# Norm factors on all partitions: one product with ones and 32x32 turns on VectorE, in place of single-column and identity products

## The chip, the cores and the metric

The kernel runs on one core of one Trainium2 chip. The metric is device time in microseconds (us) of the whole execution, as the median of three runs. Engines are named as the profile does: PE is TensorE (PEld its weight loads), DVE VectorE, ACT ScalarE, POOL GpSimd, SP SyncE.

## The reference, cut to what matters

The program is one step of a two-layer decoder for a prompt of 1024 tokens and 8 samples of 8 tokens each. All is float32. The change touches two kinds of normalisation:

```python
def rmsnorm(x, g):
    xf = x.astype(F32)
    y = xf * lax.rsqrt(jnp.mean(xf * xf, axis=-1, keepdims=True) + NORM_EPS)
    return (y * g.astype(F32)).astype(x.dtype)
...
    # end of the RWKV-7 mixer, per token and head of 64
    mean = jnp.mean(o, axis=-1, keepdims=True)
    var = jnp.mean(jnp.square(o - mean), axis=-1, keepdims=True)
    o = ((o - mean) * lax.rsqrt(var + RW_GN_EPS) * p['ln_w'].reshape(RW_HEADS, HEAD_DIM).astype(F32)
         + p['ln_b'].reshape(RW_HEADS, HEAD_DIM).astype(F32))
```

`rmsnorm` stands ahead of both mixers and both FFNs, at the end of the Mamba-2 mixer (over 512 features) and at the end of the trunk.

## The kernel before

**Layout.** Features lie on the 128 partitions and tokens along the columns; a tensor of 1024 features is eight tiles. The tokens go in two halves: one of 576 columns (64 of the samples and 512 of the prompt, worked in the groups 0 to 320 and 320 to 576) and one of 512 columns (one group). A sum over features is thus a sum over partitions, which TensorE makes by a product, and the factor that comes out has to stand on all partitions again to multiply the tiles.

**Dense work.** Weights come by DMA, ScalarE rounds them to a high part `wh` (line 196) and GpSimd, or VectorE in the middle of the program, makes the low part `wl` (line 198). The activations are split in the same way into `hh` (ScalarE, line 218) and `hl` (line 219, VectorE for even tiles and GpSimd for odd ones). `mm3` multiplies in three products (lines 204 to 206) into one of four PSUM banks of the tag `acc`.

**A norm** is `rms` (lines 226 to 258). ScalarE squares the tiles and VectorE adds them up (line 239) into `ss`. For each block of 128 tokens (five for 576 columns, four for 512) one product of `ss` with a column of ones gives the sums, a token on each partition (line 245). VectorE takes the mean and adds epsilon (line 247), GpSimd raises to -0.5 (line 224, a power, one column a block), and for each block a product of the factor with the identity writes the factor on all partitions (line 255), into one PSUM bank for each group. `rms_split` then multiplies the eight tiles by factor and gain on VectorE (line 269), with the factor read from PSUM, and splits them. `rms` is called 13 times: eight times for the norms ahead of mixers and FFNs, twice at the end of the Mamba-2 mixer (tag `rk`, line 1485) and three times at the end (line 1525).

**The recurrence.** `Unit.finish` closes each of the 17 units of the RWKV-7 recurrence (256 columns): a product with the block matrix `blk` for the means (line 813), the difference on VectorE (814), the square on ScalarE (816), two products of the squares with the two columns `blk2` (820), the mean on VectorE (822), the power on GpSimd (224), a copy that spreads the four columns over 256 (824), two products with the identity (828) and the multiplication by the factor in PSUM (830). It runs beside other units' work; all of it shares two PSUM banks of the tag `rk`.

**What sets the order.** Generators are woven by hand: dense work yields, and the recurrence, attention or the norm of the other half takes its turn. Each engine then gets one fixed order of instructions, and an engine waits at the head of its own queue, whatever stands behind.

Of the kernel before, what the change touches and what calls it, by code (L numbers as in the profile page):

```python
# [19 lines left out]
P = 128  # L20
# [65 lines left out]
CC = {}  # L86
CN = []
for _pack, _items in enumerate(((("ident", 128), ("ones", 1), ("nhalf", 1)),
                                (("blk", 128), ("blk2", 2), ("maskp", 128), ("masks", 128), ("m2", 32), ("m4", 32), ("m8", 32),
                                 ("m16", 32), ("m1t", 32), ("i32", 32), ("bsel", 8)),  # L90
                                (("causal", 128), ("ssdmp", 128), ("ssdms", 64), ("bsel1", 8)),
                                (("smask", 256), ("pgtri", 128), ("sel", 32), ("hmask", 4), ("sub", 1)))):
    _n = 0
    for _name, _w in _items:
        CC[_name] = (_pack, _n, _w)
        _n += _w
    CN.append(_n)


def shape_constants():  # L100
    c = [np.zeros((P, n), np.float32) for n in CN]

    def put(name, a):
        a = np.asarray(a, np.float32)
        pack, n, w = CC[name]
        assert a.shape[1] == w
        c[pack][: a.shape[0], n:n + w] = a
# [5 lines left out]
    put("ones", np.ones((P, 1)))  # L113
    put("nhalf", np.full((P, 1), -0.5))
    put("blk", (r[:, None] // 64) == (r[None, :] // 64))
    put("blk2", (r[:, None] // 64) == np.arange(2)[None, :])
    strict = s[:, None] < t[None, :]
    incl = s[:, None] <= t[None, :]
    same = (s[:, None] // LS) == (t[None, :] // LS)
# [107 lines left out]
def rms(k, H, xs, width, groups=None, ft=None, tag="acc"):  # L227

    nc = k.nc
    ft = ft or (lambda: k.ft(H))  # L230
    groups = groups or H.groups
    lo, hi = groups[0][0], groups[-1][1]
    blocks = [b for b in H.blocks if lo <= b[1] < hi]
    ss = ft()[:, lo:hi]
    for i, x in enumerate(xs):
        sq = ft()[:, lo:hi] if i else ss
        nc.scalar.activation(sq, x[:, lo:hi], AF.Square)
        if i:
            nc.vector.tensor_add(ss, ss, sq)  # L239
        if i % 2:  # L240
            yield
    pt = k.bank(tag)
    nb = len(blocks)
    for j, (l, _, _) in enumerate(blocks):
        nc.tensor.matmul(pt[:, j:j + 1], ss[:, l - lo:l - lo + P], k.con("ones"), start=True, stop=True)  # L245
    r = k.bp.tile([P, 16], F32, name="rs", tag="rs", bufs=2)
    nc.vector.tensor_scalar(r[:, 8:8 + nb], pt[:, :nb], 1.0 / width, EPS, op0=ALU.mult, op1=ALU.add)
    rsqrt(k, r[:, 0:nb], r[:, 8:8 + nb])
    yield
    out = []  # L250
    for a, b in groups:
        pb = k.bank(tag)
        for j, (_, c, w) in enumerate(blocks):
            if a <= c < b:
                nc.tensor.matmul(pb[:, c - a:c - a + w], r[:, j:j + 1].to_broadcast([P, P]), k.con("ident")[:, :w], start=True, stop=True)  # L255
        out.append((a, b, pb[:, :b - a]))
    yield
    return out


def rms_split(k, H, xs, gname):
# [240 lines left out]
class Unit:  # L502
# [297 lines left out]
    def finish(self):  # L800
        m, cols, n, oo = self.m, self.cols, self.n, self.oo
        k = m.k
        nc = k.nc
        V, S = nc.vector, nc.scalar
        mm = nc.tensor.matmul

        def c3(t):
            return t.rearrange("p (c s) -> p c s", s=64)

        sg = self.et("sg")  # L810
        nc.sync.dma_start(sg[:, :n], k.zd[self.H.i][12][:, self.ts])
        pm = k.bank()
        mm(pm[:, 0:256], k.con("blk"), oo, start=True, stop=True)
        V.scalar_tensor_tensor(oo, pm[:, 0:256], -1.0 / 64, oo, op0=ALU.mult, op1=ALU.add)
        s2 = self.et("s2", 2)
        S.activation(s2, oo, AF.Square)
        yield
        pv = k.bank()
        for j in range(2):
            mm(pv[:, 2 * j:2 * j + 2], s2[:, 128 * j:128 * j + 128], k.con("blk2"), start=True, stop=True)  # L820
        r = m.tile([P, 8], "gr", 2)
        V.tensor_scalar(r[:, 4:8], pv[:, 0:4], 1.0 / 64, GN_EPS, op0=ALU.mult, op1=ALU.add)
        rsqrt(k, r[:, 0:4], r[:, 4:8])
        V.tensor_copy(c3(s2), r[:, 0:4, None].to_broadcast([P, 4, 64]))
        yield
        pr = k.bank()
        for j in range(2):
            mm(pr[:, 128 * j:128 * j + 128], s2[:, 128 * j:128 * j + 128], k.con("ident"), start=True, stop=True)
        for sl, i in cols:
            V.scalar_tensor_tensor(oo[:, sl], oo[:, sl], k.col("lnw", i), pr[:, sl], op0=ALU.mult, op1=ALU.mult)  # L830
        yield
        for sl, i in cols:
            V.scalar_tensor_tensor(oo[:, sl], oo[:, sl], k.col("lnb", i), self.bv[:, sl], op0=ALU.add, op1=ALU.add)
        yield
        pg = k.bank()
        for sl, i in cols:
            mm(pg[:, sl], m.g2[:, 128 * i:128 * i + 128], sg[:, :n], start=True, stop=True)
        V.scalar_tensor_tensor(oo, oo, 0.5, pg[:, 0:256], op0=ALU.mult, op1=ALU.mult)
        for sl, i in cols:
            nc.sync.dma_start(k.ysp0[self.H.i][4 + i][:, self.ts], oo[:, sl])  # L840
# [864 lines left out]
```

## Time and profile before

| | us |
|---|---|
| median of three runs | 3342.81 (3340.84 to 3344.05) |
| the profiled execution | 3342.04 |
| its span in the profile | 3340.3 |

| engine | busy us | share of the span |
|---|---|---|
| PE | 3169.4 | 95% |
| PEld | 2666.9 | 80% |
| DVE | 1906.4 | 57% |
| ACT | 1058.7 | 32% |
| POOL | 834.7 | 25% |

A busy time is the union of an engine's instructions. TensorE's instructions overlap in the records, so two of them are told apart by their starts. A product in float32 shows as two instructions in the trace.

### The profile page before, as it was taken

Reading aid. Unit: us, or ns where it says so; the run is one execution under the profiler, and the core shown is the slowest. Engines: PE = TensorE matmul, PEld = TensorE weight load, DVE = VectorE, ACT = ScalarE, POOL = GpSimd, SP = SyncE. Lnnn points to the kernel's source line nnn. Section 1 sums busy time; section 2 is a strip of 40 time slices with the busy share of each in tenths; the row PEclk is TensorE's granted clock in tenths of the full one; section 3 lists DMA queues with packets and bytes.
Section 4 is the critical chain, followed back from the end, with each engine's and each line's share of the span. In section 5 each row is a group of like instructions: output and inputs, shape, how many; then the busy total and the mean of one; then the engine's idle time right before and its main releaser. Section 6 shows DMA issues by size and latency. Waiting matters only on the chain. (4 is left out here: it accounts for less than half of the span.)

```text
span 3340.3 us, 63263 instructions
## 1 busy us (share of the span) xinstructions
PE 3169.4 (95%) x25213; PEld 2666.9 (80%) x25213; DVE 1906.4 (57%) x3643; ACT 1058.7 (32%) x2083; POOL 834.7 (25%) x561
## 2 busy tenths in 40 slices
PE   7999999999999998999999998989999998999998
PEld 7887667777889997977677675766777776899998
DVE  6766646565544447556655457565545656554445
ACT  4333323332222223345322223332224553322222
POOL 4423333332333333301300103002010001333332
PEclk9999999999999998999999999999999999999999
DMA  5322333211122234544345656775554334232222
GB/s 178 116 59 79 87 96 118 73 59 56 51 66 83 83 108 148 191 151 135 108 135 163 199 154 213 240 221 175 172 171 138 113 110 135 87 105 81 83 83 78
DMA packets 238471, 409.20 MB, mean 123 GB/s; under 512 B 37632, under 2 KB 129664, under 8 KB 238176
## 3 DMA queue, kind: packets, MB, share of 16 engines
q10 hardware_dynamic: 63232, 218.80, 20.2%
q1 hardware_dynamic: 165584, 152.27, 15.4%
q0 software_dynamic: 9360, 34.08, 3.0%
q8 instruction: 199, 3.26, 0.4%
q14 instruction: 96, 0.79, 0.1%
HBM read 352.23 MB, written 52.81 MB: 121 GB/s over the span
## 5 line engine op out<-in xcount | busy, mean ns | idle before, releaser
L204 PE MATMUL acc<-hh,wh 128*128 128x320 f32 (+2 forms) x3720 | 1264.9, 341 | 17.6 <-ACT hh L218 14.7
L206 PE MATMUL acc<-hh,wl 128*128 128x320 f32 (+2 forms) x3720 | 1255.4, 338 | 7.4 <-POOL wl L198 6.5
L205 PE MATMUL acc<-hl,wh 128*128 128x320 f32 (+2 forms) x3720 | 1254.8, 338 | 7.2 <-DVE hl L219 5.4
L204 PEld LDWEIGHTS acc<-hh,wh 128*128 128x128 f32 x3720 | 712.3, 192 | 97.5 <-ACT hh L218 19.4
L198 POOL TENSOR_TENSOR wl<-wraw,wh 128x1024 fp32r<-128x1024 f32 x225 | 539.6, 2398 | 1000.6 <-ACT wh L196 924.7
L196 ACT CAST wh<-wraw 128x1024 fp32r<-128x1024 f32 (+1 forms) x398 | 416.0, 1045 | 1139.4 <-PE acc L205 1054.1
L206 PEld LDWEIGHTS acc<-hh,wl 128*128 128x128 f32 x3720 | 712.8, 192 | 74.7 <-issue 11.1
L205 PEld LDWEIGHTS acc<-hl,wh 128*128 128x128 f32 x3720 | 713.0, 192 | 72.1 <-DVE hl L219 9.1
L205 PE MATMUL acc<-hidl,wh 128*128 128x320 f32 (+2 forms) x1056 | 353.1, 335 | 0.6 <-DVE hidl L219 0.6
L893 DVE TENSOR_TENSOR x<-x,acc 128x320 f32<-128x320 f32 (+2 forms) x528 | 270.3, 527 | 139.1 <-PE acc L206 136.1
L206 PE MATMUL acc<-hidh,wl 128*128 128x320 f32 (+2 forms) x1056 | 349.5, 332 | 0.0
L204 PE MATMUL acc<-hidh,wh 128*128 128x320 f32 (+2 forms) x1056 | 348.9, 337 | 0.4 <-ACT hidh L218 0.4
L198 DVE TENSOR_TENSOR wl<-wraw,wh 128x1024 fp32r<-128x1024 f32 x173 | 210.9, 1219 | 145.3 <-ACT wh L196 143.2
L1297 POOL DMA_INDIRECT kv<-in_cv,vidx x64 | 75.5, 1180 | 628.8 <-DVE kt L1249 134.4
L204 PEld LDWEIGHTS acc<-hidh,wh 128*128 128x128 f32 x1056 | 198.7, 189 | 24.0 <-issue 4.2
L205 PEld LDWEIGHTS acc<-hidl,wh 128*128 128x128 f32 x1056 | 199.2, 189 | 19.1 <-issue 2.2
L206 PEld LDWEIGHTS acc<-hidh,wl 128*128 128x128 f32 x1056 | 199.5, 189 | 15.6 <-issue 1.4
L219 DVE TENSOR_TENSOR hidl<-ft,hidh 128x512 fp32r<-128x512 f32 (+2 forms) x148 | 178.7, 1207 | 55.9 <-ACT hidh L218 55.8
L881 DVE SCALAR_TENSOR_TENSOR ft<-ft,acc 128x320 f32<-128x320 f32 (+2 forms) x132 | 70.1, 531 | 213.1 <-PE acc L206 212.9
L875 DVE SCALAR_TENSOR_TENSOR ft<-ft,acc 128x320 f32<-128x320 f32 (+2 forms) x132 | 69.7, 528 | 177.0 <-ACT ft L874 176.8
L218 ACT CAST hidh<-ft 128x512 fp32r<-128x512 f32 (+2 forms) x148 | 75.1, 507 | 117.5 <-DVE ft L881 114.3
L1249 DVE STREAM_TRANSPOSE kt<-kv 128x1024 f32<-128x1024 f32 x64 | 79.3, 1239 | 33.8 <-DMA kv<-in_ck 29.9
(339 smaller groups left out, 3334.7 us busy)
## 6 DMA issues: line engine op xcount, KB each, us to landing
wraw<-in_wi ACTq DMA_DIRECT2D x100, 512.0 KB
wraw<-in_wg ACTq DMA_DIRECT2D x88, 512.0 KB
wraw<-in_wu ACTq DMA_DIRECT2D x88, 512.0 KB
wraw<-in_wd ACTq DMA_DIRECT2D x88, 512.0 KB
kv<-in_ck SPq DMA_DIRECT2D x512, 64.0 KB
wraw<-in_wo ACTq DMA_DIRECT2D x32, 512.0 KB
ka<-kp SPq DMA_DIRECT2D x48, 128.0 KB
x<-in_xT SPq DMA_DIRECT2D x16, 288.0 KB
```

The source lines that it names most:

```text
L196: nc.scalar.copy(wh, raw)
L198: k.low.tensor_sub(wl, raw, wh)
L204: mm(acc, wh, xh, start=first, stop=False)
L205: mm(acc, wh, xl, start=False, stop=False)
L206: mm(acc, wl, xh, start=False, stop=last)
L218: k.nc.scalar.copy(hh, v)
L219: (eng or k.nc.vector).tensor_sub(hl, v, hh)
L875: nc.vector.scalar_tensor_tensor(s[:, a:b], s[:, a:b], 1.0, pc, op0=ALU.add, op1=ALU.mult)
L881: nc.vector.scalar_tensor_tensor(s[:, a:b], s[:, a:b], 0.5, pu, op0=ALU.mult, op1=ALU.mult)
L893: nc.vector.tensor_add(xs[n][:, a:b], xs[n][:, a:b], acc[:, :b - a])
L1249: V.transpose(kt, kr)
L1297: nc.gpsimd.indirect_dma_start(out=v, out_offset=None, in_=A["cv"].rearrange("o (s r) c -> (o s) (r c)", r=2), in_offset=bass.IndirectOffs ...
```

## The change

In `rms` one product for each group, with ones in all 128x128 weights and `ss` as the moving side, writes the sums on every partition, a token in each column. VectorE transposes the PSUM bank in 32x32 blocks into `ss`, so that the tokens of a block of 32 stand on the 32 partitions of each quadrant, in one column. Mean and power then work on 18 columns (576 tokens) or 16 (512), all four quadrants alike, in place of five or four. `turn_back` transposes these columns, each read 32 times over, into an SBUF tile `rb`, where the factor stands on all partitions; the multiplications of lines 269, 1485 and 1525 read it from there. `finish` does the same with `blk` as the weights, and eight columns in place of four; its copy and its four small products go, and its multiplication reads SBUF. The constant `blk2` goes.

```diff
-    pt = k.bank(tag)
-    nb = len(blocks)
-    for j, (l, _, _) in enumerate(blocks):
-        nc.tensor.matmul(pt[:, j:j + 1], ss[:, l - lo:l - lo + P], k.con("ones"), start=True, stop=True)
-    r = k.bp.tile([P, 16], F32, name="rs", tag="rs", bufs=2)
-    nc.vector.tensor_scalar(r[:, 8:8 + nb], pt[:, :nb], 1.0 / width, EPS, op0=ALU.mult, op1=ALU.add)
-    rsqrt(k, r[:, 0:nb], r[:, 8:8 + nb])
+
+    nb = (hi - lo) // 32
+    for a, b in groups:
+        pt = k.bank(tag)
+        nc.tensor.matmul(pt[:, :b - a], k.con("ones").to_broadcast([P, P]), ss[:, a - lo:b - lo], start=True, stop=True)
+        nc.vector.transpose(ss[:, a - lo:b - lo], pt[:, :b - a])
+    r = k.bp.tile([P, 36], F32, name="rs", tag="rs", bufs=2)
+    nc.vector.tensor_scalar(r[:, 18:18 + nb], ss[:, 0::32], 1.0 / width, EPS, op0=ALU.mult, op1=ALU.add)
+    rsqrt(k, r[:, 0:nb], r[:, 18:18 + nb])
     yield
-    out = []
-    for a, b in groups:
-        pb = k.bank(tag)
-        for j, (_, c, w) in enumerate(blocks):
-            if a <= c < b:
-                nc.tensor.matmul(pb[:, c - a:c - a + w], r[:, j:j + 1].to_broadcast([P, P]), k.con("ident")[:, :w], start=True, stop=True)
-        out.append((a, b, pb[:, :b - a]))
+    rb = k.bp.tile([P, 576], F32, name="rb", tag="rb", bufs=1)
+    turn_back(k, rb[:, 0:hi - lo], r[:, 0:nb])
     yield
-    return out
+    return [(a, b, rb[:, a - lo:b - lo]) for a, b in groups]
+
+
+def turn_back(k, out, r):
+
+    n = out.shape[1] // 32
+    k.nc.vector.transpose(out.rearrange("p (b s) -> p b s", s=32), r[:, :, None].to_broadcast([P, n, 32]))
...
         pv = k.bank()
-        for j in range(2):
-            mm(pv[:, 2 * j:2 * j + 2], s2[:, 128 * j:128 * j + 128], k.con("blk2"), start=True, stop=True)
-        r = m.tile([P, 8], "gr", 2)
-        V.tensor_scalar(r[:, 4:8], pv[:, 0:4], 1.0 / 64, GN_EPS, op0=ALU.mult, op1=ALU.add)
-        rsqrt(k, r[:, 0:4], r[:, 4:8])
-        V.tensor_copy(c3(s2), r[:, 0:4, None].to_broadcast([P, 4, 64]))
+        mm(pv[:, 0:256], k.con("blk"), s2, start=True, stop=True)
+        V.transpose(s2, pv[:, 0:256])
+        r = m.tile([P, 16], "gr", 2)
+        V.tensor_scalar(r[:, 8:16], s2[:, 0::32], 1.0 / 64, GN_EPS, op0=ALU.mult, op1=ALU.add)
+        rsqrt(k, r[:, 0:8], r[:, 8:16])
         yield
-        pr = k.bank()
-        for j in range(2):
-            mm(pr[:, 128 * j:128 * j + 128], s2[:, 128 * j:128 * j + 128], k.con("ident"), start=True, stop=True)
+        turn_back(k, s2, r[:, 0:8])
         for sl, i in cols:
-            V.scalar_tensor_tensor(oo[:, sl], oo[:, sl], k.col("lnw", i), pr[:, sl], op0=ALU.mult, op1=ALU.mult)
+            V.scalar_tensor_tensor(oo[:, sl], oo[:, sl], k.col("lnw", i), s2[:, sl], op0=ALU.mult, op1=ALU.mult)
```

The order of instructions moves with it. On TensorE at the first norm of the program (576 columns), before; `acc_324` and `acc_328` are the banks of the factor, `acc_378` and `acc_411` those of the first dense tile:

```order
L245 MATMUL acc_315<-con0_222,ft_246 128x1 x5
L255 MATMUL acc_324<-con0_222,rs_321 128x64
L255 MATMUL acc_324<-con0_222,rs_321 128x128 x2
L255 MATMUL acc_328<-con0_222,rs_321 128x128 x2
L204 MATMUL acc_378<-hh_230,wh_374 128x320
L204 MATMUL acc_411<-hh_230,wh_374 128x256
L205 MATMUL acc_378<-hl_238,wh_374 128x320
L206 MATMUL acc_378<-hh_230,wl_376 128x320
```

The same place after (lines of the changed kernel: 203 to 205 are 204 to 206 of before); `wh_484` is the weight of a second dense tile:

```order
L244 MATMUL acc_315<-ft_246,con0_222 128x320
L244 MATMUL acc_318<-ft_246,con0_222 128x256
L203 MATMUL acc_373<-hh_230,wh_369 128x320
L203 MATMUL acc_406<-hh_230,wh_369 128x256
L203 MATMUL acc_488<-hh_230,wh_484 128x320
L203 MATMUL acc_521<-hh_230,wh_484 128x256
L204 MATMUL acc_373<-hl_238,wh_369 128x320
L205 MATMUL acc_373<-hh_230,wl_371 128x320
```

The two banks of the factor are gone from the norm, and a second dense tile, which before could begin only when one of them was free again, begins with the first.

On VectorE at the end of a unit of the first recurrence, before; `gr` is the factor, `s_3878` the tile of the squares, the other rows belong to the next units:

```order
L822 TENSOR_SCALAR gr<-rk 128x4
L558 SCALAR_TENSOR_TENSOR cum<-reset,e 128x256
L824 COPY s_3878<-gr 128x256
L568 TENSOR_TENSOR e<-cum,e 128x256
L665 TENSOR_TENSOR tt<-tt,rk 128x128
```

The same place after (569, 657 and 666 are 568, 656 and 665 of before, 820 and 825 are 822 and 830):

```order
L818 STREAM_TRANSPOSE s_3862<-rk 128x256
L666 TENSOR_TENSOR tt<-tt,rk 128x128
L820 TENSOR_SCALAR gr<-s_3862 128x8
L569 TENSOR_TENSOR e<-cum,e 128x256
L657 STREAM_TRANSPOSE t_4143<-tt 128x128
L666 TENSOR_TENSOR tt<-tt,rk 128x128
L259 STREAM_TRANSPOSE s_3862<-gr 128x256
L818 STREAM_TRANSPOSE s_3928<-rk 128x256
L657 STREAM_TRANSPOSE t_4164<-tt 128x128
L820 TENSOR_SCALAR gr<-s_3928 128x8
L825 SCALAR_TENSOR_TENSOR oo<-oo,pp,s_3862 128x256
```

One instruction stood between the mean and what waits for the power; now there are three, and the multiplication follows on VectorE alone, four rows later.

On VectorE at the end of the program (the last 256 columns of the trunk's last norm), before, from the mean of the first group on:

```order
L247 TENSOR_SCALAR rs<-acc 128x3
L239 TENSOR_TENSOR ft<-ft 128x256
L893 TENSOR_TENSOR x<-x,acc 128x256
L239 TENSOR_TENSOR ft<-ft 128x256
L1525 SCALAR_TENSOR_TENSOR x<-x,pp,acc 128x320 x2
L893 TENSOR_TENSOR x<-x,acc 128x256 x2
L1525 SCALAR_TENSOR_TENSOR x<-x,pp,acc 128x320 x6
L239 TENSOR_TENSOR ft<-ft 128x256 x3
L247 TENSOR_SCALAR rs<-acc 128x2
L1525 SCALAR_TENSOR_TENSOR x<-x,pp,acc 128x256 x8
```

And after (237, 888 and 1520 are 239, 893 and 1525 of before):

```order
L245 STREAM_TRANSPOSE ft<-acc 128x320
L237 TENSOR_TENSOR ft<-ft 128x256
L247 TENSOR_SCALAR rs<-ft 128x10
L888 TENSOR_TENSOR x<-x,acc 128x256
L259 STREAM_TRANSPOSE rb<-rs 128x320
L888 TENSOR_TENSOR x<-x,acc 128x256
L1520 SCALAR_TENSOR_TENSOR x<-x,pp,rb 128x320
L888 TENSOR_TENSOR x<-x,acc 128x256
L1520 SCALAR_TENSOR_TENSOR x<-x,pp,rb 128x320 x7
L237 TENSOR_TENSOR ft<-ft 128x256 x3
L245 STREAM_TRANSPOSE ft<-acc 128x256
L247 TENSOR_SCALAR rs<-ft 128x8
```

Two turns came in for each of the two groups, and the second of them, which needs the power, stands on VectorE ahead of the last two additions.

## Rows read from the trace of the kernel before

**Rows 1.** The page of the profile: its span, and busy time of each engine with its share of the span and its instructions.

```profile
span 3340.3 us, 63263 instructions
...
PE 3169.4 (95%) x25213; PEld 2666.9 (80%) x25213; DVE 1906.4 (57%) x3643; ACT 1058.7 (32%) x2083; POOL 834.7 (25%) x561
```

**Rows 2.** Busy time by stretch (from:to, length, then busy us and instructions of TensorE, its weight loads, VectorE, ScalarE and GpSimd; granted clock of TensorE, DMA share, GB/s). 40 to 960 holds the two recurrences; 960 to 1255 is dense work alone.

```profile
40.00:960.00 920.00, 863.70 (x10402) 707.19 (x10401) 557.54 (x1398) 296.36 (x733) 301.08 (x237) 0.96 0.27 82
960.00:1255.00 295.00, 295.00 (x2168) 291.81 (x2167) 127.74 (x218) 73.49 (x110) 110.60 (x46) 1.00 0.27 89
```

**Rows 3.** The waits of TensorE (line waited for: us in total, times, longest us).

```profile
PE acc L255 <- POOL rs L224: 12.1, 8, 2.4
...
PE rk L828 <- DVE s L824: 3.7, 3, 2.8
...
PE rk L255 <- POOL rs L224: 2.8, 2, 1.7
```

**Rows 4.** The timeline of all engines at the norm of the last FFN, 2880 to 2900 (start us, us, engine, line, operation, tiles, shapes, count; in brackets the idle time ahead and what ended it).

```profile
2883.05 2.47 DVE L239 TENSOR_TENSOR ft<-ft 128x576 f32<-128x576 f32 x1 [1.13 <-ACT ft L237]
...
2885.58 2.29 PE L245 MATMUL acc<-con,ft 128*128 128x1 f32 x10 [4.11 <-DVE ft L239]
2887.91 0.17 DVE L247 TENSOR_SCALAR rs<-acc 128x5 f32<-128x5 f32 x1 [2.38 <-PE acc L245]
2888.15 1.17 POOL L224 TENSOR_TENSOR rs<-rs,con 128x5 f32<-128x5 f32 x1 [3.24 <-DVE rs L247]
...
2891.06 0.55 DVE L269 SCALAR_TENSOR_TENSOR ft<-x,pp,acc 128x320 f32<-128x320 f32 x1 [2.99 <-PE acc L255]
...
2893.83 1.78 DVE L269 SCALAR_TENSOR_TENSOR ft<-x,pp,acc 128x320 f32<-128x320 f32 x4
...
2894.03 1.42 POOL L219 TENSOR_TENSOR hl<-ft,hh 128x576 fp32r<-128x576 f32 x1 [4.71 <-ACT hh L218]
...
2896.20 1.78 DVE L269 SCALAR_TENSOR_TENSOR ft<-x,pp,acc 128x320 f32<-128x320 f32 x4
```

**Rows 5.** The products of one norm and of one recurrence unit on TensorE's own timeline, with the engine busy on both sides (columns as in rows 4). A product in float32 stands as two rows' worth: x8 are four products. Rows overlap, so what one takes from the engine is read from start to start.

```profile
2928.42 0.95 PE L245 MATMUL acc<-con,ft 128*128 128x1 f32 x8
2929.23 0.39 PE L204 MATMUL acc<-hidh,wh 128*128 128x320 f32 x1
...
2935.68 1.05 PE L255 MATMUL acc<-con,rs 128*128 128x128 f32 x8
2936.49 0.39 PE L204 MATMUL acc<-hh,wh 128*128 128x320 f32 x1
...
224.58 0.59 PE L813 MATMUL rk<-oo,con 128*128 128x256 f32 x2
225.01 1.05 PE L622 MATMUL rk<-krz,kb 128*128 128x128 f32 x8
```

**Rows 6.** The reciprocal square roots on GpSimd, line 224: min/median/max ns, the first and the last start, and the forms.

```profile
L224 POOL TENSOR_TENSOR gr<-gr,con x17: 1006/1016/1336, 240.9 to 949.2; 128x4 f32<-128x4 f32 x17
L224 POOL TENSOR_TENSOR rs<-rs,con x13: 695/1047/2101, 21.1 to 3331.4; 128x4 f32<-128x4 f32 x6, 128x5 f32<-128x5 f32 x5, 128x3 f32<-128x3 f32 x1, 128x2 f32<-128x2 f32 x1
```

**Rows 7.** Groups of VectorE by line and shape: the 32x32 transposes that are there already, and two lines of the unit's end (count | busy us, mean ns | idle ahead, and what ended it).

```profile
L1249 DVE STREAM_TRANSPOSE kt<-kv 128x1024 f32<-128x1024 f32 x64 | 79.3, 1239 | 33.8 <-DMA kv<-in_ck 29.9 <-issue 2.9 <-DMA kp<-hidh 1.0
...
L656 DVE STREAM_TRANSPOSE t<-tt 128x128 f32<-128x128 f32 x66 | 19.2, 299 | 0.4
...
L824 DVE COPY s<-gr 128x256 f32<-128x256 f32 x17 | 9.3, 549 | 13.4 <-POOL gr L224 13.4
...
L830 DVE SCALAR_TENSOR_TENSOR oo<-oo,pp,rk 128x256 f32<-128x256 f32 x16 | 7.6, 478 | 6.3 <-PE rk L828 6.1
```

**Rows 8.** VectorE's timeline at three norms of 512 columns: the last sum of squares, and the first product with the factor (columns as in rows 4).

```profile
1514.56 0.68 DVE L239 TENSOR_TENSOR ft<-ft 128x512 f32<-128x512 f32 x1
...
1518.91 0.75 DVE L269 SCALAR_TENSOR_TENSOR ft<-x,pp,acc 128x512 f32<-128x512 f32 x1 [1.98 <-PE acc L255]
...
2033.36 0.68 DVE L239 TENSOR_TENSOR ft<-ft 128x512 f32<-128x512 f32 x1
...
2039.28 1.41 DVE L269 SCALAR_TENSOR_TENSOR ft<-x,pp,acc 128x512 f32<-128x512 f32 x2 [3.29 <-issue]
...
2286.90 0.68 DVE L239 TENSOR_TENSOR ft<-ft 128x512 f32<-128x512 f32 x1
...
2294.34 0.75 DVE L269 SCALAR_TENSOR_TENSOR ft<-x,pp,acc 128x512 f32<-128x512 f32 x1 [5.45 <-PE acc L255]
```

**Rows 9.** VectorE's timeline at the end of the program (columns as in rows 4).

```profile
3324.04 1.01 DVE L1525 SCALAR_TENSOR_TENSOR x<-x,pp,acc 128x320 f32<-128x320 f32 x2 [1.07 <-PE acc L255]
...
3328.55 1.47 DVE L239 TENSOR_TENSOR ft<-ft 128x256 f32<-128x256 f32 x3
...
3333.45 3.22 DVE L1525 SCALAR_TENSOR_TENSOR x<-x,pp,acc 128x256 f32<-128x256 f32 x8 [2.09 <-PE acc L255]
```

**Rows 10.** Two lines of VectorE with min/median/max ns, line 269 (one input in PSUM) and line 365 (both in SBUF); and an addition of two SBUF tiles beside a subtraction of GpSimd on the timeline of all engines.

```profile
L269 DVE SCALAR_TENSOR_TENSOR ft<-x,pp,acc x96: 461/538/748, 24.0 to 2899.9; 128x320 f32<-128x320 f32 x32, 128x256 f32<-128x256 f32 x32, 128x512 f32<-128x512 f32 x32
...
L365 DVE SCALAR_TENSOR_TENSOR ft<-up,pp,ft x16: 731/748/2719, 153.1 to 1258.5; 128x512 f32<-128x512 f32 x16
...
2876.17 2.41 POOL L198 TENSOR_TENSOR wl<-wraw,wh 128x1024 fp32r<-128x1024 f32 x1 [3.99 <-ACT wh L196]
...
2876.66 2.54 DVE L239 TENSOR_TENSOR ft<-ft 128x576 f32<-128x576 f32 x1 [1.12 <-ACT ft L237]
```

More of the change, by code (lines that the diff above doesn't have):

```diff
@@ L88 @@
 for _pack, _items in enumerate(((("ident", 128), ("ones", 1), ("nhalf", 1)),
-                                (("blk", 128), ("blk2", 2), ("maskp", 128), ("masks", 128), ("m2", 32), ("m4", 32), ("m8", 32),
+                                (("blk", 128), ("maskp", 128), ("masks", 128), ("m2", 32), ("m4", 32), ("m8", 32),
                                  ("m16", 32), ("m1t", 32), ("i32", 32), ("bsel", 8)),
@@ L115, in shape_constants @@
     put("blk", (r[:, None] // 64) == (r[None, :] // 64))
-    put("blk2", (r[:, None] // 64) == np.arange(2)[None, :])
     strict = s[:, None] < t[None, :]
@@ L232, in rms @@
     lo, hi = groups[0][0], groups[-1][1]
-    blocks = [b for b in H.blocks if lo <= b[1] < hi]
     ss = ft()[:, lo:hi]
@@ L805, in finish @@
         mm = nc.tensor.matmul
-        def c3(t):
-            return t.rearrange("p (c s) -> p c s", s=64)
         sg = self.et("sg")
```

## The prediction

> **What bounds the kernel now.** I read the page first. TensorE is busy for 3169.4 of 3340.3 us, VectorE for 1906.4 [rows 1]: TensorE sets the time, and an edit counts by what it takes out of TensorE's own row or out of its gaps, 171 us in all. The busy time by stretch says where the gaps are: none in 295 us of dense work alone, 920.0 - 863.7 = 56 us in the two recurrences, where the ends of the 17 units lie [rows 2]. The rest is at norms and at the end of the program. The waits of TensorE name the edited lines: 12.1 us at the identity products of the norms for GpSimd's power, 2.8 us at those of the two Mamba norms, 3.7 us in the units for the spreading copy [rows 3]. Then the timeline of one norm that nothing covers [rows 4]: from the end of the last addition (2883.05 + 2.47 = 2885.52) to the first multiplication with the factor at 2891.06 pass 5.54 us, through TensorE, VectorE, GpSimd and TensorE again, and no dense work can start. Such a chain counts by its length, not by the work in it. So there are three kinds of places: norms beside other work, norms that are bare, and the units.
>
> **The products, beside other work.** With TensorE busy on both sides, eight instructions of the single-column products take 2929.23 - 2928.42 = 0.81 us and eight of the identity products 0.81 us, as their starts show [rows 5]: a single column costs what 128 columns cost. One product of 256 columns takes 225.01 - 224.58 = 0.43 us, so 512 columns take 0.86 and 576 take 0.97 by the same rate. A norm of 512 columns goes from 1.62 to 0.86 us (saves 0.76), one of 576 from ten and ten instructions, 2.02, to 0.97 (saves 1.05). Five norms have dense work on both sides (near 68, 664, 1692, 2820 and 2929 us): 3 x 0.76 + 2 x 1.05 = 4.4 us. At 1692 and 2820, the Mamba norms, nothing on TensorE needs the factor any more, so their 2.8 us of waiting go too [rows 3]. Sum: **-7.2 us**.
>
> **The units.** Eight instructions (0.81 us) become one product of 256 columns (0.43): 17 x 0.38 = 6.5 us. TensorE's 3.7 us of waiting for the copy go, since the factor no longer passes through it. Against that stands VectorE, whose results the same units wait for. The power costs GpSimd 0.695 us for the fewest columns, two, 1.006 at least for four [rows 6], 1.17 for five [rows 4]; that is a line, about 0.39 + 0.155 a column, so eight columns take 1.63, sixteen 2.87 and eighteen 3.18 us. No row shows more than five columns. The bounds are 1.17 (no growth) and 3.2 (the line); I take the line, since all shapes lie near it. A transpose takes 0.299 us for 128 and 1.239 for 1024 columns [rows 7], so 0.17 + 1.05 ns a column: 0.44 for 256, 0.50 for 320, 0.70 for 512, 0.77 for 576. None here reads PSUM or one column 32 times over; a multiplication with an input in PSUM runs 0.738 us for 512 columns and one of SBUF alone 0.748 at the median (lines 269 and 365), so I take the same price, and 0 to twice as the bound. VectorE now spends on the units 9.3 us in copies, 13.4 waiting for the power and 6.3 waiting for the identity products [rows 7], 29 us. After: two transposes, 17 x 0.88 = 15 us, and a wait for the power of 1.63 + 0.1, less two instructions of other units that stand between on average (about 0.6 us), 17 x 1.1 = 19 us. That is 34 us, 5 more. VectorE is at six tenths in this stretch (557.5 of 920 us, [rows 2]), so I let half of it reach TensorE: +2.5 us, between 0 and 5. Sum: -6.5 - 3.7 + 2.5 = **-7.7 us**.
>
> **The bare norms.** Six chains stand bare: 576 columns near 21, 1264 and 2888 us, 512 near 1516, 2036 and 2289. At 2888 TensorE runs at half pace (2.29 us for ten instructions, [rows 4]), so the new chain is: gap 0.06, products 2 x 0.97 = 1.94, gap and the second transpose 0.49 (the first lies under the second product), gap and mean 0.22, gap and power 0.07 + 3.18, gap and turn 0.05 + 0.77. That makes 6.8 us against 5.54. Before, the second group came 0.4 us behind the first, and now both are there at once, so the first finished tile is late by +0.8 us; I take this for all three. For 512 columns at full pace: 0.06 + 0.86 + 0.75 + 0.22 + 2.94 + 0.75 = 5.6 us. The old chains, from the last addition's end to the first multiplication, were 3.67 (1515.24 to 1518.91), 5.24 (half pace: 6.4 against it) and 6.76 us, where GpSimd and other products stood between [rows 8]: +1.9, +1.2, -1.1. At the end VectorE itself is the path. It waited 1.07 us for the factor of the first group [rows 9]. Now it makes two turns of 320 columns (0.84 in sequence) and waits about 1.5 for a power of ten columns (1.94): +1.3. For the last group a product at half pace (0.86), 0.49, 0.22, power of eight 1.70, turn 0.49 make 3.8 us against 3.43 (3328.55 + 1.47 = 3330.02 to 3333.45): +0.3. Sum: 2.4 + 2.0 + 1.6 = **+6.0 us**. If the power did not grow, the same sum would be about -6.
>
> **The place of the factor.** It moves from PSUM to SBUF. Line 269 with the factor in PSUM never took over 748 ns in 96 runs; line 365, both inputs in SBUF, has a median of 748 and a longest of 2719 ns, and a VectorE addition of two SBUF tiles took 2.54 us beside a GpSimd subtraction of 2.41 [rows 10]. So the multiplications become stoppable by GpSimd, which in each of eight norms makes four subtractions of `hl` (1.42 us at 2894.03, [rows 4]) while VectorE multiplies. The Trainium skill has this as a rule ("SBUF — State Buffer", "Who interferes with whom"): a VectorE instruction with two SBUF inputs and a GpSimd instruction that reads SBUF exclude each other for a whole instruction. The trace agrees with it by the two rows just named; it is the rule that speaks against this change, and the time by it is the first rival's. Against it stands the order on TensorE: the factor's banks are free, a second dense tile starts at once, and so TensorE has twice the work for each `hl` that comes. I put **+2 us** on it.
>
> **Sum:** -7.2 - 7.7 + 6.0 + 2 = -6.9 us on 3342.04, the profiled execution: 3335.1. That run lies 0.77 under the median of the three, so 3335.9; I say **3336**.
>
> **Rivals.** *VectorE stopped by GpSimd decides; slower.* A pair of tiles leaves the norm every 2896.20 - 2893.83 = 2.37 us [rows 4]; with a subtraction of 1.42 in line it is 3.8. Dense work takes TensorE 295.00 / 2168 = 0.136 us a product [rows 2]; a pair is 12 products in one dense tile, 1.6 us of work, and 3.2 in two. If the second tile's weights are not there in time, TensorE waits; at half of 4 x 1.42 in six norms that is 17 us: 3336 + 17 = 3353. For it: the durations in [rows 10]; against it: the order on TensorE, and TensorE at half pace after such a gap. It decides from the point where a pair takes longer than the tiles in hand. *The power is nearly flat; clearly faster.* At 1.17 us the bare norms gain 12 us, the units some 4 more: 3320. For it: from three to four columns it grew little; against it: two to five columns. The PSUM banks that come free would add to this. *The units don't feel it.* If the recurrences are paced by their own chain and not by TensorE's queue, the -7.7 goes and the rest is +0.8: about 3343.
>
> **How the numbers follow.** A run of this kernel can tell about 0.2% (6.7 us, so 3336.1 and 3349.5) from no change. The forecast, with 3328 to 3344 around it, has a chance of 0.50, and as its middle lies on the line it gives 0.28 to faster and 0.22 to the same. The stopped VectorE has 0.23 (0.18 slower, 0.05 same), the flat power 0.17 (faster), the units that don't feel it 0.10 (same). Faster 0.45, same 0.37, slower 0.18. The range reaches to the middles of the outer rivals: 3318 to 3353.
>
> **What the profile of after would show.** The power of 16 and 18 columns at 2.9 and 3.2 us, of eight at 1.6. Chains from the last addition to the first multiplication of 6.8 and 5.6 us. No wait of TensorE at a power. Transposes of 0.44 to 0.77 us. TensorE's busy time down by 6 us or more in 40 to 960, with gaps of 56 us or less. The forecast is wrong if the power is under 2 us, if multiplications at line 269 stretch to 1.5 us and more with TensorE waiting for `hl` behind them, or if the gaps in 40 to 960 grow by what the products save.

## The result, and the profile after

The changed kernel takes 3376.55 us (median of four runs, 3375.67 to 3384.03) where the kernel before takes 3342.57 beside it: ratio 1.0107, 95% interval 1.0089 to 1.0124, so slower by 34 us. The forecast was 3336, with a range up to 3353: the sign was wrong and the time lies outside the range.

The page of the changed kernel, as in [rows 1]:

```profile
span 3374.6 us, 62708 instructions
...
PE 3138.9 (93%) x24931; PEld 2634.5 (78%) x24931; DVE 1948.8 (58%) x3691; ACT 1059.6 (31%) x2083; POOL 876.4 (26%) x561
```

TensorE's busy time did fall, by 30.5 us. But its gaps grew from 170.9 us to 3374.6 - 3138.9 = 235.7: the work that was taken out was replaced by more than twice as much waiting.

Busy time by stretch, columns as in [rows 2]. The recurrences now lie at 52.7 to 974.3, the dense work alone behind them:

```profile
52.70:974.30 921.60, 847.30 (x10220) 690.02 (x10219) 568.37 (x1413) 293.17 (x727) 315.29 (x235) 0.96 0.26 81
974.30:1269.10 294.80, 294.31 (x2163) 290.81 (x2162) 128.46 (x220) 73.97 (x112) 110.69 (x46) 1.00 0.28 89
```

Dense work alone is as it was. In the recurrences TensorE has 74.3 us of gaps in place of 56.3.

The norm of the last FFN, timeline of all engines (start us, us, engine, line, operation, tiles, shapes, count; idle time ahead), against [rows 4]:

```profile
2908.88 2.47 DVE L237 TENSOR_TENSOR ft<-ft 128x576 f32<-128x576 f32 x1 [1.12 <-ACT ft L235]
...
2911.41 2.29 PE L244 MATMUL acc<-ft,con 128*128 128x320 f32 x4 [4.11 <-DVE ft L237]
...
2913.73 0.45 DVE L245 STREAM_TRANSPOSE ft<-acc 128x256 f32<-128x256 f32 x1 [0.34 <-PE acc L244]
2914.22 0.18 DVE L247 TENSOR_SCALAR rs<-ft 128x18 f32<-128x18 f32 x1
2914.47 3.21 POOL L223 TENSOR_TENSOR rs<-rs,con 128x18 f32<-128x18 f32 x1 [3.74 <-DVE rs L247]
2917.72 0.78 DVE L259 STREAM_TRANSPOSE rb<-rs 128x576 f32<-128x576 f32 x1 [3.32 <-POOL rs L223]
2918.53 1.80 DVE L270 SCALAR_TENSOR_TENSOR ft<-x,pp,rb 128x320 f32<-128x320 f32 x4
...
2920.92 2.95 DVE L270 SCALAR_TENSOR_TENSOR ft<-x,pp,rb 128x320 f32<-128x320 f32 x4
2921.11 1.62 POOL L218 TENSOR_TENSOR hl<-ft,hh 128x576 fp32r<-128x576 f32 x1 [3.43 <-ACT hh L217]
...
2924.46 2.97 DVE L270 SCALAR_TENSOR_TENSOR ft<-x,pp,rb 128x320 f32<-128x320 f32 x4
...
2924.66 1.64 POOL L218 TENSOR_TENSOR hl<-ft,hh 128x576 fp32r<-128x576 f32 x1 [1.93 <-ACT hh L217]
```

Two things are to be seen. The chain from the last addition (2911.35) to the first multiplication (2918.53) takes 7.18 us in place of 5.54. And a pair of tiles takes 2924.46 - 2920.92 = 3.54 us in place of 2.37: the four multiplications, 1.78 us before, take 2.95 whenever GpSimd makes its subtraction. TensorE's waits at this norm, before (2885.5 to 2912) and after (2911 to 2940); line, waited for, us in all, times, longest us:

```profile
PE acc L255 <- POOL rs L224: 1.5, 1, 1.5
PE acc L204 <- ACT hh L218: 1.3, 1, 1.3
PE acc L205 <- POOL hl L219: 0.2, 1, 0.2
...
PE acc L203 <- ACT hh L217: 6.5, 1, 6.5
...
PE acc L204 <- POOL hl L218: 1.8, 3, 0.9
PE acc L205 <- POOL wl L197: 1.3, 1, 1.3
```

The one wait for `hh` holds the rest of the chain. The stopped multiplications reach TensorE behind it, in waits for what GpSimd makes: 1.8 + 1.3 us in place of 0.2.

Durations by line (ns, min/median/max): the power, the multiplication with the factor, the turn back:

```profile
L223 POOL TENSOR_TENSOR gr<-gr,con x17: 1633/1646/1803, 254.5 to 970.6; 128x8 f32<-128x8 f32 x17
L223 POOL TENSOR_TENSOR rs<-rs,con x13: 1634/2935/4147, 21.8 to 3365.6; 128x16 f32<-128x16 f32 x6, 128x18 f32<-128x18 f32 x5, 128x10 f32<-128x10 f32 x1, 128x8 f32<-128x8 f32 x1
...
L270 DVE SCALAR_TENSOR_TENSOR ft<-x,pp,rb x96: 470/546/2794, 25.8 to 2930.5; 128x320 f32<-128x320 f32 x32, 128x256 f32<-128x256 f32 x32, 128x512 f32<-128x512 f32 x32
...
L259 DVE STREAM_TRANSPOSE s<-gr x17: 445/445/449, 256.2 to 972.2; 128x256 f32<-128x256 f32 x17
L259 DVE STREAM_TRANSPOSE rb<-rs x13: 445/712/779, 25.0 to 3367.3; 128x512 f32<-128x512 f32 x6, 128x576 f32<-128x576 f32 x5, 128x320 f32<-128x320 f32 x1, 128x256 f32<-128x256 f32 x1
```

Of the 96 multiplications of line 270, 18 take over 0.9 us, 14 of them at the six bare norms; before, none took over 0.75 [rows 10].

Waits of TensorE in the whole kernel before, where [rows 7] has VectorE's:

```profile
PE acc L204 <- ACT hh L218: 14.7, 9, 4.1
...
PE rk L639 <- DVE t L656: 7.0, 9, 1.7
```

Waits of TensorE and of VectorE after:

```profile
PE acc L203 <- ACT hh L217: 31.7, 9, 7.3
PE rk L640 <- DVE t L657: 15.9, 12, 3.5
...
DVE rb L259 <- POOL rs L223: 37.7, 13, 3.5
...
DVE s L259 <- POOL gr L223: 23.1, 17, 3.4
```

No wait of TensorE names the power any more. VectorE stands at it instead: 23.1 us in the units where the copy stood 13.4 [rows 7]. TensorE feels it one step on, at `t`, a transpose that VectorE makes for the next units: 15.9 us in place of 7.0.

**Where the time goes**, by place. I matched TensorE's instructions of two traces, the n-th of a line and its tiles with the n-th, and took the median difference of their starts in stretches of 25 us of the kernel before; the last column is the difference of the spans. The other kernels are those of the next section.

| us later than before | at 100 | 950 | 1225 | 1325 | 2850 | 2950 | end |
|---|---|---|---|---|---|---|---|
| changed kernel | 12.7 | 14.3 | 14.1 | 19.6 | 25.8 | 32.8 | 34.3 |
| norms_only | 10.7 | 5.2 | 5.0 | 9.2 | 15.7 | 24.2 | 26.0 |
| norms_psum | 2.0 | 1.9 | 1.7 | 2.4 | 11.2 | 11.4 | 13.4 |
| before_sbuf | 8.6 | 0.0 | -0.1 | 1.0 | 2.6 | 6.1 | 6.8 |
| units_only | 0.4 | 6.0 | 5.9 | 7.5 | 11.6 | 11.6 | 13.2 |
| before_pow8 | 0.0 | 7.6 | 7.6 | 7.7 | 9.0 | 8.3 | 9.4 |
| units_psum | 1.0 | -17.8 | -17.9 | -16.0 | -9.0 | -9.4 | -7.9 |

In the changed kernel the first norm costs 12.7 us, the one near 1264 5.5, the two near 2888 and 2929 together 7.0. The recurrences look innocent (12.7 to 14.3). The experiments show that they are not: norms_only and before_sbuf, late by 9 to 11 us after the first norm, win 5.5 to 8.6 of it back there, and the new units' ends take that away.

Two things limit this table. Each row is a single execution, and 34 of the kernel before on one chip lie between 3329.1 and 3355.3 us, with mean granted clocks of 0.978 to 0.972. And TensorE's clock is not the same in all rows. At the upper of its two levels two products of 320 columns start 0.15 us apart (2901.71 and 2901.86 in the kernel before), at the lower 0.27 (2894.40 and 2894.67), so, as an estimate from these two, a us of TensorE's work at the lower level loses about 0.45 us. By the trace's record of the granted clock TensorE worked, in the whole kernel, 144 us at the lower level before and 149 after: that is 2 of the 34 us, so the clock does not explain the result. Between 40 and 980 us it matters:

| 40 to 980 us | before | changed | norms_only | before_sbuf | units_only | before_pow8 | units_psum | units_pv |
|---|---|---|---|---|---|---|---|---|
| TensorE's work at the lower level, us | 67 | 69 | 56 | 52 | 71 | 62 | 47 | 98 |

By this estimate 5 of the 5.5 us that norms_only wins back in the recurrences, and 6.5 of the 8.6 of before_sbuf, are a higher clock, and so are some 9 of units_psum's 19 there. before_pow8 loses its 7.6 with less of the lower level than before. No run holds the clock fixed, so whether an edit moves it or the execution does is not shown.

### The profile page after: what moved, and what is told of

It is laid out like the page before. It is cut to its first block, busy times and chain, and to the rows that moved or that the text cites. A ratio compares the mean times of both kernels' runs of the same rounds, so it can differ in the third digit from the quotient of the medians.

```text
span 3374.6 us, 62708 instructions
## 1 busy us (share of the span) xinstructions
PE 3138.9 (93%) x24931; PEld 2634.5 (78%) x24931; DVE 1948.8 (58%) x3691; ACT 1059.6 (31%) x2083; POOL 876.4 (26%) x561
## 4 chain that ended last, share of the span: by engine, by line
PE 56%; DVE 5%; issue 5%; DMA 5%; POOL 2%; ACT 1%; SPq 1%; POOLq 0%; DVEq 0%; ACTq 0%
PE acc L203 16%; PE acc L204 16%; PE acc L205 16%; DMA kv<-in_cv,vidx 1%; PE rk L1177 1%; PE rk L1285 1%; PE fs L1249 1%; PE fs L1150 1%; DVE ft L270 1%; PE rk L1169 1%; DMA ac<-acd 1%; POOL wl L197 1%; POOL rs L223 1%; DVE ft L1338 1%; ACT wh L195 1%
## 5 line engine op out<-in xcount | busy, mean ns | idle before, releaser
L203 PE MATMUL acc<-hh,wh 128*128 128x320 f32 (+3 forms) x3720 | 1260.4, 341 | 35.6 <-ACT hh L217 31.7
L204 PE MATMUL acc<-hl,wh 128*128 128x320 f32 (+3 forms) x3720 | 1255.0, 338 | 11.2 <-POOL hl L218 5.9
L205 PE MATMUL acc<-hh,wl 128*128 128x320 f32 (+3 forms) x3720 | 1252.4, 338 | 11.8 <-POOL wl L197 11.4
L203 PEld LDWEIGHTS acc<-hh,wh 128*128 128x128 f32 (+1 forms) x3720 | 712.5, 192 | 116.2 <-ACT hh L217 39.4
L205 PEld LDWEIGHTS acc<-hh,wl 128*128 128x128 f32 (+1 forms) x3720 | 713.5, 192 | 76.6 <-POOL wl L197 13.9
L204 PEld LDWEIGHTS acc<-hl,wh 128*128 128x128 f32 (+1 forms) x3720 | 713.9, 192 | 75.6 <-DVE hl L218 10.2
L205 PEld LDWEIGHTS acc<-hidh,wl 128*128 128x128 f32 x1056 | 199.9, 189 | 15.2 <-issue 1.6
L1404 POOL TENSOR_TENSOR ac<-ac,bc 128x576 f32<-128x576 f32 (+1 forms) x16 | 23.4, 1476 | 304.8 <-ACT ac L1403 304.7
```

Of the source, the lines that this page charges most:

```text
L203: mm(acc, wh, xh, start=first, stop=False)
L204: mm(acc, wh, xl, start=False, stop=False)
L205: mm(acc, wl, xh, start=False, stop=last)
```

## The experiments

The theory after the result: the norms lose by multiplications that GpSimd stops, since their factor stands in SBUF. Its rival: the longer chain, with the power of 16 and 18 columns, is the loss. For the units the question was open. All ratios are to the kernel before on the same chip; 0.1% is 3.3 us.

**The parts alone.** units_only is the kernel before with the new `finish`; norms_only has the new `rms` and the old `finish`.

> The kernel before with the units' ends alone in the new form (one product with blk, turn, power of eight columns, turn back); the norms keep single columns and identity products. By the prediction's term for the units (-7.7 us) this gives 3335 us. By the rival that the units don't feel it, and by the shift between the two traces, which stays between 12.7 and 14.3 us over the whole stretch of the recurrences, it gives 3342 to 3345, with TensorE busy some 6 us less in 40 to 960 and its gaps as much longer.

> The changed kernel with the units' ends in the old form; the norms keep the row sums, turns, the power of 16 or 18 columns and the factor in SBUF. If the norms alone make the change slower, as the shift between the traces says (12.7 us at the first norm, 5.5 at the one near 1264, 7 at the two near 2888 and 2929, about 6 between), it gives 3372 to 3377. If the units cost the time, it gives 3345 or less.

Measured: units_only 1.0040 (1.0025 to 1.0055), norms_only 1.0086 (1.0070 to 1.0102). Both parts are slower. The units cost 13 us, more than either expectation, and their -7.7 falls. Waits of units_only in 40 to 980:

```profile
DVE s L264 <- POOL gr L224: 23.4, 17, 3.4
...
PE rk L645 <- DVE t L662: 17.1, 13, 3.5
```

**The factor's place, taken away and added.** factor_psum turns the norms' factor into PSUM; before_sbuf copies the old factor into SBUF.

```diff
 factor_psum
-    turn_back(k, rb[:, 0:hi - lo], r[:, 0:nb])
+    for a, b in groups:
+        pb = k.bank(tag)
+        turn_back(k, pb[:, :b - a], r[:, (a - lo) // 32:(b - lo) // 32])
 before_sbuf (behind the identity products; rb is an SBUF tile)
+        nc.scalar.copy(rb[:, a - lo:b - lo], pb[:, :b - a])
...
-        out.append((a, b, pb[:, :b - a]))
+        out.append((a, b, rb[:, a - lo:b - lo]))
```

> The changed kernel, but the norms' second turn writes PSUM banks, one a group, so the multiplication with the factor reads one input in PSUM again. Theory 1, GpSimd's subtractions and VectorE's multiplications of two SBUF tiles stop each other: a pair of tiles goes from 3.55 us back to 2.37, four pairs a norm, so up to 4.7 us in each of six bare norms and what hangs behind the first: 3345 to 3355 us. Theory 2, the chain with the power of 18 columns costs the time: pairs shrink or not, the total stays at 3370 to 3378.

> The kernel before, whole in its chain (single columns, power of five columns, identity products), with one step added: ScalarE copies each group's factor from PSUM to SBUF and the multiplications read it there. Theory 1: pairs of tiles go from 2.37 to 3.55 us at the norms, six bare norms lose 4 to 4.7 us each beside the copy's half us, and the first some more: 3365 to 3378 us. Theory 2: only the copies, about 0.5 us a bare norm and their hop: 3345 to 3350.

Measured: factor_psum 1.0073 (1.0055 to 1.0090), before_sbuf 1.0047 (1.0030 to 1.0064). VectorE's timeline at the last FFN's norm in factor_psum:

```profile
2907.14 0.85 DVE L262 STREAM_TRANSPOSE acc<-rs 128x320 f32<-128x320 f32 x2 [3.33 <-POOL rs L223]
2907.90 1.75 DVE L273 SCALAR_TENSOR_TENSOR ft<-x,pp,acc 128x320 f32<-128x320 f32 x4
2909.57 0.75 DVE L218 TENSOR_TENSOR hl<-ft,hh 128x576 fp32r<-128x576 f32 x1
2910.23 1.79 DVE L273 SCALAR_TENSOR_TENSOR ft<-x,pp,acc 128x320 f32<-128x320 f32 x4
...
2912.60 1.78 DVE L273 SCALAR_TENSOR_TENSOR ft<-x,pp,acc 128x320 f32<-128x320 f32 x4
```

And the timeline of all engines at the same norm in before_sbuf:

```profile
2896.54 2.95 DVE L271 SCALAR_TENSOR_TENSOR ft<-x,pp,rb 128x320 f32<-128x320 f32 x4
2896.74 1.61 POOL L219 TENSOR_TENSOR hl<-ft,hh 128x576 fp32r<-128x576 f32 x1 [5.13 <-ACT hh L218]
...
2900.08 2.96 DVE L271 SCALAR_TENSOR_TENSOR ft<-x,pp,rb 128x320 f32<-128x320 f32 x4
```

The pair is 2.37 us with the factor in PSUM and the new chain, 3.54 with it in SBUF and the old chain. So the place alone sets it. before_sbuf loses 16 us by the medians (7 by the spans), less than theory 1's 23 and more than theory 2's 7. That is not the place alone, for with ScalarE's copies its six bare chains are 0.1 to 1.2 us longer than before, 3.6 in all. And the place is not the whole loss: factor_psum stays 24 us over, where 12 at most were expected; against the changed kernel, the same but for the place, it gains 11 us by the ratios and 17 by the spans.

**The chain alone.** norms_psum is norms_only with the factor in PSUM. norms_psum_pow5 is factor_psum with the power of five columns; the first column's factor goes to all tokens:

```diff
-    rsqrt(k, r[:, 0:nb], r[:, 18:18 + nb])
+    rsqrt(k, r[:, 0:5], r[:, 18:23])
...
-        turn_back(k, pb[:, :b - a], r[:, (a - lo) // 32:(b - lo) // 32])
+        turn_back(k, pb[:, :b - a], r[:, 0:1].to_broadcast([P, (b - a) // 32]))
```

> The norms alone in the new form, their factor turned into PSUM, the units' ends as in the kernel before. If the factor's place in SBUF was the greater part of norms_only's 29 us (pairs of 3.55 in place of 2.37 us at six norms, about 17 us) and the longer chain (7.1 to 5.5 us, 5.9 to 3.7 to 6.8) the smaller, it lies 5 to 13 us over the kernel before. If the chain is the greater part, 15 us or more over it.

> factor_psum with the norms' power taken of five columns only and the first column's factor turned back for all (most columns get a wrong factor): the power falls from 2.95 to 3.22 us to 1.2. If the power's length counts in full at the six bare norms, 5 x 2.0 + 1.75 or so, the run lies 9 to 13 us under factor_psum (that was 23 us over the kernel before, so 10 to 14 over it). If other work stands between, or the norm is paced by its pairs, it lies within 4 us of factor_psum.

Measured: norms_psum 1.0039 (1.0025 to 1.0053), 13 us, at the upper edge of the first expectation; norms_psum_pow5 0.9986 (0.9972 to 0.9999), 29 us under factor_psum by the ratios and 3357.4 - 3346.4 = 11 us by the spans. But the execution behind that span took 3348.19 where the median of its kernel is 3337.17, so the ratios weigh more, and they say much more than the 9 to 13 expected. The power's length counts; why it counts for so much, in a kernel that still has units_only's ends, stays open. Place and chain are about equal parts of the norms' loss by the ratios: 29 - 13 = 16 us and 13.

**The units: wait or place?** In units_only four of the 20 multiplications with the factor meet GpSimd's weight subtraction. One of them, all engines:

```profile
516.06 0.45 DVE L264 STREAM_TRANSPOSE s<-gr 128x256 f32<-128x256 f32 x1 [1.75 <-POOL gr L224]
516.54 3.01 DVE L830 SCALAR_TENSOR_TENSOR oo<-oo,pp,s 128x64 f32<-128x64 f32 x4
516.67 2.40 POOL L198 TENSOR_TENSOR wl<-wraw,wh 128x1024 fp32r<-128x1024 f32 x1 [0.65 <-ACT wh L196]
```

So both theories have a place there: A, VectorE stands at the longer power; B, the multiplications are stopped. The edits, each on units_only:

```diff
 units_pow4
-        rsqrt(k, r[:, 0:8], r[:, 8:16])
+        rsqrt(k, r[:, 0:4], r[:, 8:12])
-        turn_back(k, s2, r[:, 0:8])
+        turn_back(k, s2, r[:, 0:1].to_broadcast([P, 8]))
 units_psum (and the multiplication reads pr)
-        turn_back(k, s2, r[:, 0:8])
+        pr = k.bank()
+        turn_back(k, pr[:, 0:256], r[:, 0:8])
 units_pv (and the multiplication reads pv)
+        turn_back(k, pv[:, 256:512], r[:, 0:8])
 units_psum_copy (units_psum, and the multiplication reads s2)
+        S.copy(s2, pr[:, 0:256])
 units_y3 (ahead of turn_back)
+        yield
+        yield
+        yield
```

> units_only with the power taken of four columns, as in the kernel before, and the first column's factor turned back for all 256: the other 224 columns of a unit get a wrong factor, the instructions are as many and as large but for the power, 1.02 us in place of 1.64. Theory A, VectorE stands at the head of its queue for the longer power and TensorE waits behind it: VectorE's wait falls from 23 us to 13 or less, TensorE's wait for t from 17 to 7 to 10, and the run lies 0 to 7 us under the kernel before. Theory B, the factor of the units in SBUF, or the order of instructions as such: it stays 10 to 14 us over it, as units_only.

> units_only with the second turn written to a PSUM bank, so the multiplication with the factor reads one input in PSUM, as in the kernel before; the power keeps eight columns. Theory B, GpSimd and VectorE stop each other there: 0 to 5 us from the kernel before. Theory A: stays 8 to 14 us over it.

> units_only with three more pauses between the power and the turn back, so that VectorE has more instructions of other units in its queue between the two (a middle of 5 in place of 2). Theory A: VectorE's 23 us of waiting for the power fall under 10 and the run lies 0 to 7 us under the kernel before. Theory B: no gain over units_only.

> units_only with the second turn written to the free half of the bank that held the sums: the factor stands in PSUM, and the turn keeps its place in VectorE's queue (0 to 5 instructions behind the mean, as in units_only; in units_psum there were 7 to 21). If the multiplications stopped by GpSimd cost the time, they show no duration over 0.7 us, VectorE's wait for the power stays near 23 us, and the run comes close to units_psum, 8 to 18 us under the kernel before. If the late place of the turn brought units_psum's gain, it stays 5 to 14 us over the kernel before, as units_only.

> units_psum with one step more: ScalarE copies the turned factor from PSUM to SBUF and the multiplication reads it there; the turn keeps its late place. If the late place alone brings the gain, 8 to 18 us under the kernel before. If the SBUF input costs it, some multiplications take 2 to 2.6 us again and the run lies from 3 under to 12 over.

| kernel | ratio (interval) | VectorE waits for the power, us | TensorE waits for `t`, us | longest multiplication, ns |
|---|---|---|---|---|
| before | 1 | 13.4 | 7.0 | 482 |
| units_only | 1.0040 (1.0025 to 1.0055) | 23.4 | 17.1 | 2567 |
| units_pow4 | 0.9997 (0.9982 to 1.0011) | 12.9 | 12.9 | 485 |
| units_pv | 1.0066 (1.0049 to 1.0084) | 23.8 | 15.6 | 481 |
| units_psum | 0.9955 (0.9941 to 0.9969) | 6.9 | 5.7 | 482 |
| units_psum_copy | 0.9991 (0.9976 to 1.0006) | 6.9 | 6.4 | 2110 |
| units_y3 | 1.0041 (1.0027 to 1.0054) | 15.1 | 12.6 | 2379 |

The waits of VectorE at the power in units_pow4, units_pv and units_psum, 40 to 980:

```profile
DVE s L264 <- POOL gr L224: 12.9, 15, 2.8
...
DVE rk L264 <- POOL gr L224: 23.8, 17, 3.4
...
DVE rk L264 <- POOL gr L224: 6.9, 3, 3.4
```

units_pow4 has units_only's order of instructions on TensorE, VectorE and ScalarE; with the shorter power the loss is gone. By itself that does not tell A from B: its multiplications came at other moments than GpSimd's subtractions, none took over 485 ns, and so both causes went at once. units_pv has the factor in PSUM and no stopped multiplication, but the full wait, and is slower than units_only, 22 us over the kernel before where 14 at most were expected (it also keeps its bank longer, and its trace has the most work at the lower clock; which of them adds to the wait was not tried). units_psum met neither expectation, 15 us under where A said over. Its gain comes with a new place of the turn: it stands 7 to 21 instructions behind the mean in 14 of the 17 units, and VectorE seldom waits for the power (that the turn waits for one of the two banks is argued from the code). units_psum_copy keeps that place with the factor in SBUF. Four of its multiplications take 1.4 to 2.1 us again, and it lies 3 us under the kernel before, 12 slower than units_psum: the outcome named for the SBUF input, with ScalarE's copy in it. (By the spans, 3330.5 and 3332.4, the two are alike, but the execution behind the span of units_psum took 3334.17 where its median is 3327.77.) So neither the late place nor PSUM alone brings the 15 us. A is a cause by units_pv, which has the wait and no stopped multiplication, and by before_pow8 below; B is worth 12 us at most. units_y3 was a miss: its wait fell only to 15.1 us, and nothing was gained.

**The power in the old form.** before_pow8 takes mean and power of eight columns, each of the four twice, in the kernel before; before_late3 puts four pauses ahead of its spreading copy and takes out the one behind it.

```diff
 before_pow8
-        rsqrt(k, r[:, 0:4], r[:, 4:8])
...
+        rsqrt(k, r[:, 0:8], r[:, 8:16])
 before_late3
+        yield
+        yield
+        yield
+        yield
         V.tensor_copy(c3(s2), r[:, 0:4, None].to_broadcast([P, 4, 64]))
-        yield
```

> The kernel before with one edit in the units' ends: mean and power are taken of eight columns (each of the four twice), so the power takes 1.64 us in place of 1.02; copy, products and outputs as before. If VectorE standing at the power is what makes units_only slower, its wait goes from 13.4 to about 23 us, TensorE's waits in the recurrences grow, and the run lies 5 to 14 us over the kernel before. If the turns or the missing products are the cause, within 4 us of it.

> The kernel before with three more pauses between the power and the spreading copy in the units' ends, the old form otherwise: the copy has a middle of 3 instructions between itself and the mean, up to 12, in place of 2. If a late place by itself brings what units_psum gained, it lies 5 us or more under the kernel before. If not, within 4 us of it.

Measured: before_pow8 1.0045 (1.0029 to 1.0061), before_late3 1.0071 (1.0052 to 1.0090). Waits of before_pow8 in 40 to 980:

```profile
DVE s L824 <- POOL gr L224: 24.0, 17, 1.8
...
PE rk L639 <- DVE t L656: 13.0, 10, 2.9
```

0.63 us more of power in 17 units, no turn and no missing product, bring the whole loss of units_only: 15 us by the medians, 9 by the spans. before_late3 shows the limit of this theory: VectorE's wait fell to 8.0 us, and the kernel is 24 us slower. So less standing at the power does not by itself make the kernel faster. Pauses put all the later steps of a unit off; what in that costs so much was not followed.

**Both factors in PSUM.** both_psum is the changed kernel with the edits of factor_psum and units_psum.

> The changed kernel with both factors in PSUM: factor_psum's norms and units_psum's ends. If the two parts add up (norms in PSUM, from units_only to factor_psum, +4 to +11 us; units in PSUM -15), it lies 2 to 12 us under the kernel before and over units_psum. If they don't add, units_psum's gain is lost in it: within 3 us of the kernel before or slower.

Measured: 0.9983 (0.9971 to 0.9996), 6 us under the kernel before and over units_psum, as expected (by the spans it is the shorter, 3329.1 against 3332.4 us, so their order rests on the ratios). The version that beats both kernels by most is units_psum: old norms, new units' ends with their factor in PSUM, 15 us (10 to 20) faster than the kernel before.

## Why the prediction was wrong

**What was right.** The prices: the power at 1.63, 2.94 and 3.21 us (forecast 1.63, 2.87, 3.18), the turns back at 0.45 to 0.78 (0.44 to 0.77), the bare chains at 6.9 to 7.2 us for 576 columns (6.8) and 5.9 to 6.9 for 512 (5.6). TensorE has no wait at a power. Its busy time in the recurrences fell by 16.4 us. And two of the signs named for a wrong forecast came true: multiplications with the factor took 1.5 us and more with TensorE waiting for `hl` behind them, and the gaps in the recurrences grew by 18.0, more than the products saved.

**The step that failed most: the place of the factor, +2 us.** The first rival had the mechanism, and its 17 us were near: 16 us by norms_only against norms_psum, 11 by the changed kernel against factor_psum (13 and 17 by the spans). Its total of 3353 was not, since it kept the other terms. It got 0.23 because of the argument that a second dense tile gives TensorE twice the work for each `hl`. By the prediction's own numbers that is 3.2 us of work a pair at full pace, and the pair measured 3.54: two tiles in hand are not enough. At the norm near 2888 the later dense work moved by 30.5 - 25.8 = 4.7 us: the chain's 7.18 - 5.54 = 1.64, and 3.1 of the 3 x 1.17 by which the pairs are longer, as much as the waits for `hl` and `wl` there grew (1.8 + 1.3 - 0.2). With the factor in PSUM the same place moved by 16.4 - 15.2 = 1.2 us. At the first norm the delay also reaches what hangs behind it: 12.7 us in the changed kernel, 2.2 in factor_psum.

**The units: "half of it reach TensorE", +2.5 us.** VectorE's wait was sized well (19 us forecast, 23.1 measured). But VectorE at six tenths busy was read as slack, and it is not slack for an instruction that stands at the head of its queue while `t` and the rest of the next units wait behind it. before_pow8 adds 10.6 us of standing and costs 15 (10 to 20; 9 by the spans); all of it arrives, or nearly. Whether the 6.5 us of products came out is not settled: units_pow4, with them removed and the old power's length, equals the kernel before within -6 and +4 us by the medians, while its trace is 4.9 us shorter. Measured +13 in place of -7.7.

**The covered norms, -7.2, and the bare ones, +6.0.** Together -1.2; norms_psum, which is these two terms without the place, measured +13 (8 to 18). TensorE is busy on both sides of a covered norm, but what waits for that norm is late by its chain all the same: the one near 664 took 28.48 us from its last addition to its first multiplication in norms_psum against 18.45 before, 21.61 in norms_psum_pow5. Most of norms_psum's loss comes between 1325 and 2850 (2.4 to 11.2 us); the three bare norms there explain 2.3 + 1.7 - 0.3 = 3.7 us by their chains. The other 5 need no cause in the norms: in the same stretch units_psum, whose code there is that of the kernel before, moved by 7.0 us and units_only by 4.1, so single executions differ by as much.

**The sum.** 13 (units) + 16 (place) + 13 (chain) = 42 us by the medians, against 34 to 36 for the whole change. The difference is within the intervals of these runs (some 5 us each way). The parts may overlap too, since part of a delay at the first norm is won back in the recurrences, by the estimate above for the most part through the clock; no run tests it. (The range's lower end, 3318, lies 2 us under the 3320 of the rival whose middle it should be; nothing hangs on it.)

## What to carry to other kernels

When an operation leaves an engine that sets the time for one with slack, price it by what stands behind it in the new engine's queue, not by that engine's busy share: 0.63 us in 17 places was 9 to 15 us. Look where the result will stand before looking at the instruction count: a factor moved from PSUM to SBUF made every multiplication with it stoppable by GpSimd, and 18 of the 96 at the norms were stopped. And a better form can be hidden by a worse place in the queue: the same units' ends were 0.40% slower or 0.45% faster by where the turn stood and what it wrote.

## What the runs showed of the hardware

A multiplication on VectorE with both inputs in SBUF and a GpSimd subtraction shut each other out: one of each four took up to 1.65 us where none takes over 0.55 with the factor in PSUM, and the subtraction grew from 1.42 to 1.62 us. The Trainium skill ("SBUF — State Buffer", "Who interferes with whom") says that a VectorE instruction with two SBUF inputs contends with a GpSimd one that reads SBUF; the 3.54 and 2.37 us agree, in both directions of the test. That each shuts the other out for a whole instruction, as the prediction has it, that section states outright only for VectorE's two-port modes; here a stopped multiplication takes 1.62 to 1.65 us beside subtractions of 1.61 to 1.64, which fits it. A turn that reads each column 32 times over costs what a plain one does, 0.445 us for 256 columns against 0.440 at the median, and writing PSUM costs much the same (two turns of 320 and 256 columns in 0.85 us, one of 576 into SBUF in 0.78). GpSimd's power goes on at some 0.16 us a column, 1.63 for eight to 3.21 for eighteen.
